# A hybrid decoder block on one core: the order of the FFN's products, where P2 of a block stands and when its sum is added

## The chip, the cores and the metric

One core of one Trainium2 chip runs the whole block in one launch. The metric is the device time of one execution in microseconds. Below, PE is TensorE, DVE VectorE, ACT ScalarE, POOL GpSimd and SP SyncE, whose queue starts nearly all DMAs.

## The reference, cut to what matters

The block is a decoder layer over 1024 tokens of width 1024. Its first part (two kinds of linear attention, an output projection, layer norms) is not touched. The part that matters is the second, a gated MLP whose up-projection is followed by a causal convolution of three taps along the tokens:

```python
def conv_ffn(h, w_up, conv_w, conv_b, w_down):
    u = causal_dwconv(h @ w_up, conv_w) + conv_b
    gate, val = jnp.split(u, 2, axis=-1)
    return (jax.nn.silu(gate) * val) @ w_down

x = layer_norm(ALPHA * x + (1.0 + gt_a) * y, ln1_g[l], ln1_b[l])
h = x * (1.0 + sc_f) + sh_f
y = conv_ffn(h, ffn_w_up[l], ffn_conv[l], ffn_conv_b[l], ffn_w_down[l])
x = layer_norm(ALPHA * x + (1.0 + gt_f) * y, ln2_g[l], ln2_b[l])
```

`w_up` is 1024 x 5632 (2816 gate columns, 2816 value columns), `w_down` 2816 x 1024, all in float32.

## The kernel before, in words

Float32 products are made of three matmuls each: every operand is split into a high and a low part (`hi`, `lo`; ACT casts the high part, DVE or POOL subtracts it to get the low one), and PE adds hi x lo, lo x hi and hi x hi. On top of that a product of 2 x 2 blocks is made with seven block products P1 to P7 in place of eight, whose operands and results are sums of blocks.

**First product (up).** `w_up` is worked through in 22 blocks f = 0 to 21, each of 128 gate columns and 128 value columns. `product(f, i)` (L1281) is 12 matmuls of 128x512. A block has two PSUM tiles named `up`, `gp[f]` for the gate and `vp[f]` for the value, each with two halves of 512 columns and two buffers, so that `gp[f]` reuses the buffer of `gp[f-2]`. P1, P6 and P7 go to half 1 of `gp[f]`, P2 to half 0; P5 and P3 go to half 0 of `vp[f]`. P4 of block f goes on top of P7 in half 1 of `gp[f]` and is computed only in the middle of block f+1. "A pair" below is the stretch in which PE does P1(f), P5(f), P4(f-1) and the other four products of f.

`carry` does what follows each product on the other engines. Behind P1, P5 and P6 an ACT copy puts the bank into SBUF cells (`p1_`, `p5_`, `u2_`; L1471, L1473, L1475). `add_p1` (L1458, DVE) adds the copy of P1 to half 0 of `gp[f]`, where P2 lies. Behind P3 and P7 come DVE sums (L1479, L1481), behind P7 also the value's convolution: one ACT pass (L1400) and two DVE passes (L1403). Behind P4(f-1) `gate_end(f-1)` does the gate's convolution (the same three passes), the silu (ACT, L1462) and the multiply of gate and value (DVE, L1463, 1024 columns). A wait is for a whole tile: a product that writes half 1 of `gp[f]` also waits for an `add_p1(f)` that was issued ahead of it and touches half 0 only. P2 waits for the copy `p1_`, P7 for the copy `u2_`.

The weights of block f+1 are prepared meanwhile. `load_w` starts the DMAs (L1326, L1327 for the value, L150 in `gate_block` for the gate, 512 KB). `weights` forms the sums on DVE (L1333, L1336, L1346, L1347) and splits them (`split_q`, L1306). `split_w` splits the gate's block: an ACT cast (L157, into `whi`) and a POOL subtraction over 1024 columns (L158, into `wlo`); `whi` and `wlo` have two buffers, which P1 and P2 of a block read, P2 last. Every second pair `sums` forms the operands of the second product and stores them to DRAM (`put_split`: L1410 cast, L1411 subtraction, L1412 and L1413 stores); `residual_rows` works on the residual (L1451, L1452).

**The first seam.** `h2_of(t)` makes row block t of the FFN's input: PE transposes (L1224), then ACT and DVE (L1231 to L1245) scale, split and sum them. P1 and P2 of blocks 0 and 1 are computed between the last of these, then P4(0), P5(0) and so on, whose left operands (`s1h` to `s4l`, L1362 and L1363) are sums over all row blocks.

**Second product (down).** The same seven products, 11 steps each, all steps of one product before the next, in `ORDER`. `b_of` loads and forms the right operand in `R0`, `R1` or the ring `bt`; `collect` takes each finished product out of PSUM. P4 comes last, and `ln2` does the last layer norm on row blocks.

The order of PE's instructions is written out by hand (`seq`, `ORDER`). On the other engines a scheduler orders the instructions when the program is built, so the place of a DVE instruction is read from the built program and not from the source. `tc.issue_after` fixes single instructions behind another.

Of the kernel before, what the change touches and what calls it, by code (L numbers as in the profile page):

```python
# [16 lines left out]
ALU = mybir.AluOpType  # L17
# [8 lines left out]
NT = 8  # L26
DFF = 2816
NF = DFF // P
# [59 lines left out]
def build(ctx, tc, out, cst, x, c, ln0_g, ln0_b, w_ada, b_ada, w_in, dn_conv, dn_a_log, dn_dt_bias,  # L88
# [1198 lines left out]
    with tc.manual_schedule(engines={PE.engine}):  # L1287
        for t in range(NT):
            y_half(t, 1)
            ln1(t)  # L1290
            if t >= LAG:
                h2_of(t - LAG)
        raw = {0: gate_block(0), 1: gate_block(1)}
        product(0, 1)
        product(0, 2)
    mix.close()
# [68 lines left out]
    with tc.manual_schedule(engines={PE.engine}):  # L1365
# [3 lines left out]
        next(ahead)  # L1369
        h2_of(NT - 2)  # L1370
        product(1, 1)
        next(ahead)
        for i, tag in ((5, "s1"), (6, "s2"), (3, "s4"), (7, "s3")):
# [4 lines left out]
            opA[i] = (lambda k, hl=parts_s[i]: tuple(a[:, :, ct(k)] for a in hl))  # L1378
        h2_of(NT - 1)
        product(1, 2)  # L1380
        for i in (5, 6):
# [56 lines left out]
    def residual_rows(n):  # L1438

        hf, t = n // NT, n % NT  # L1440
        if t == 0:
            for box, v, tag in ((g1h, ln1_g, "g1h"), (b1h, ln1_b, "b1h")):
                box[0] = ft([P, 512], tag, 1)
                nc.sync.dma_start(box[0], v[0][HS[hf]].partition_broadcast(P))
                S.mul(box[0], box[0], ALPHA)
        r = r_cells[n % 2]
# [7 lines left out]

    pending, anchor = [], [None]

# [10 lines left out]
    def carry(f, i):  # L1467
# [4 lines left out]
        elif i == 5:  # L1472
            S.copy(p5_, v[:, 0, :])  # L1473
        elif i == 6:
            S.copy(u2_, g[:, 1, :])  # L1475
        elif i == 2 and f < NF - 1:
            add_p1(f)
# [21 lines left out]
    with tc.manual_schedule(engines={PE.engine}):  # L1499
# [11 lines left out]
        for f in range(1, NF):  # L1511
            more = f + 1 < NF
            if f == 1:
                seq = (5, 6, 3, 7)
            elif more:
                seq = (2, -4, 6, 3, 7)
            else:
                seq = (-4, 6, 3, 7, 2)
# [40 lines left out]
    R0 = fr.tile([P, NJ, 512], F32, tag="R0", name="R0")  # L1559
    ORDER = (1, 5, 6, 3, 7, 2, 4)  # L1560
    SPARE = (NJ - 3, NJ - 2, NJ - 1)
# [6 lines left out]
    def b_of(i, j):  # L1568

        r0, r1 = R0[:, j, :], R1_[0][:, j, :] if R1_ else None  # L1570
        if i in (6, 3):
            b = dt_([P, 512], "bt", 6)
            load_b(b, j, 1, 1)
            if i == 3:
                return b
            V.tensor_tensor(r1, b, r1, op=ALU.subtract)
            return r1
        if i == 1:
            load_b(r0, j, 0, 0)
        elif i == 2:  # L1580
            load_b(r0, j, 1, 0)
        elif i == 5:
# [3 lines left out]
        elif i == 7:  # L1586
            V.tensor_tensor(r0, r1, r0, op=ALU.subtract)
        else:
            V.tensor_tensor(r0, r0, r1, op=ALU.subtract)
        return r0  # L1590
# [39 lines left out]
    def matmuls(pb, i, j, t, cols=slice(0, 512)):  # L1630
        hi, lo = ents[i, j]
        l_hi, l_lo, r_hi, r_lo = hi[:, ct(t)], lo[:, ct(t)], hi[:, HS[1]][:, cols], lo[:, HS[1]][:, cols]
        new = i in (1, 5, 2) and j == 0
        PE.matmul(pb, l_hi, r_lo, start=new, stop=False, skip_group_check=i not in (1, 5, 2))  # L1634
        PE.matmul(pb, l_lo, r_hi, start=False, stop=False, skip_group_check=i not in (1, 5, 2))  # L1635
        PE.matmul(pb, l_hi, r_hi, start=False, stop=(j == NJ - 1), skip_group_check=i not in (1, 5, 2))  # L1636

# [37 lines left out]
    def collect(i, t, pb):  # L1675
# [4 lines left out]
        elif i == 6:  # L1680
            S.copy(c12(t), pb)
        elif i == 3:
            done(c12(t), pb, HS[1], res[t, 1], c12(t))
            stats(t, HS[1], 512)
        elif i == 7:
            done(c22(t), pb, HS[1], res[t + 4, 1], c22(t))
            stats(t + 4, HS[1], 512 if t < 3 else 256)
        elif i == 2:
            done(c11(t), pb, HS[0], res[t, 0], c11(t))
            stats(t, HS[0], 512)  # L1690
            ln2(t, 2, CUT_EARLY)

    steps = [(i, j) for i in ORDER for j in range(NJ)]
    AHEAD = 5
    with tc.manual_schedule(engines={PE.engine}):
# [6 lines left out]
        for i in ORDER[:-1]:  # L1702
            pbs = on5 if i in (5, 3, 2) else on1
            for j in range(NJ):
                if n < len(steps):
                    entry(*steps[n])
                    n += 1
                if i == 3 and j == 0:
                    ln2_rows.extend(rows_of(2, ln2_g[0], ln2_b[0]))
# [41 lines left out]
```

## Time and profile before

| | us |
|---|---|
| median of 3 runs | 1446.52 (1445.31 to 1451.27) |
| profiled execution | 1447.39, of which the span is 1445.7 |
| PE busy | 1337.2 (92%) |
| DVE busy | 1005.0 (70%) |
| ACT busy | 590.1 (41%) |
| POOL busy | 532.9 (37%) |

Times below are counted from the start of the span. Busy time includes time in which a started instruction is held up by something else on the chip. The mean granted clock of TensorE was 0.956 of full speed.

### The profile page before, as it was taken

How to read it: one execution, taken by the hardware profiler on the slowest of the kernel's cores; microseconds unless marked ns; L12 is line 12 of the kernel's file. 1: busy time of each engine (PE TensorE's matmuls, PEld its weight loads, DVE VectorE, ACT ScalarE, POOL GpSimd, SP SyncE). 2: the span in 40 equal slices, each digit the busy share in tenths (PEclk: the TensorE clock that was granted, in tenths of full speed). 3: DMA queues.
4: the chain of work that ended last, by engine and by line, in shares of the span. 5: the costliest groups of instructions: out<-in, count | busy, mean ns of one | idle time of the engine just before them, and what ended most of it. 6: DMA issues, size and time to landing. Idle time of an engine off the chain costs nothing.

```text
span 1445.7 us, 19012 instructions
## 1 busy us (share of the span) xinstructions
PE 1337.2 (92%) x6662; PEld 1061.9 (73%) x6662; DVE 1005.0 (70%) x1770; ACT 590.1 (41%) x957; POOL 532.9 (37%) x369
## 2 busy tenths in 40 slices
PE   6796999999999899999988989999899998999995
PEld 4564768787887678777866767777687786788885
DVE  7885955487547432794497768877988887732777
ACT  4356222233234332352565444454544544353222
POOL 2674311122115667352323433444444331342006
PEclk9898999999999999899999999999999998999998
DMA  9557212122203464253132343445444438975773
GB/s 316 148 157 208 65 32 59 32 68 57 58 23 102 139 190 146 88 189 117 78 113 80 103 140 126 143 160 189 148 143 160 153 119 307 391 243 162 266 252 117
DMA packets 195572, 209.15 MB, mean 145 GB/s; under 512 B 30099, under 2 KB 125199, under 8 KB 195477
## 3 DMA queue, kind: packets, MB, share of 16 engines
q1 hardware_dynamic: 195189, 206.89, 44.5%
q8 instruction: 53, 0.87, 0.3%
q10 hardware_dynamic: 288, 1.05, 0.2%
q14 instruction: 42, 0.34, 0.1%
HBM read 149.92 MB, written 57.97 MB: 144 GB/s over the span
## 4 chain that ended last, share of the span: by engine, by line
PE 50%; DVE 23%; DMA 10%; issue 9%; POOL 4%; ACT 3%; SPq 1%; POOLq 0%; DVEq 0%; ACTq 0%
PE up L1281 9%; PE pp L622 6%; PE pp L623 5%; PE pp L624 5%; PE up L1634 4%; PE up L1636 4%; PE up L1635 4%; DMA vq<-in_ffn_w_up 3%; DVE ob L1403 2%; DVE vq L1333 1%; POOL vl L1306 1%; PE dn L864 1%; DVE mac L236 1%; DMA K<-in_w_ada 1%; DVE vl L1306 1%
## 5 line engine op out<-in xcount | busy, mean ns | idle before, releaser
L622 PE MATMUL pp<-aH,wlo 128*128 128x512 f32 x432 | 190.9, 442 | 8.8 <-DVE ob L651 6.4
L158 POOL TENSOR_TENSOR wlo<-wst,whi 128x1024 fp32r<-128x1024 f32 x50 | 122.6, 2452 | 160.0 <-ACT whi L157 159.5
L624 PE MATMUL pp<-aH,whi 128*128 128x512 f32 x432 | 176.8, 409 | 0.0
L623 PE MATMUL pp<-aL,whi 128*128 128x512 f32 x432 | 176.7, 409 | 0.0
L1306 POOL TENSOR_TENSOR vl<-vq,vh 128x512 fp32r<-128x512 f32 x44 | 70.2, 1595 | 213.3 <-ACT vh L1305 209.0
L1634 PE MATMUL up<-aL,aH 128*128 128x512 f32 (+1 forms) x304 | 118.7, 391 | 11.8 <-DVE ob L1669 7.1
L1403 DVE SCALAR_TENSOR_TENSOR ob<-up,colC,ob 128x1023 f32<-128x1023 f32 (+1 forms) x88 | 112.2, 1276 | 20.8 <-ACT ob L1400 19.5
L1635 PE MATMUL up<-aH,aL 128*128 128x512 f32 (+1 forms) x304 | 118.2, 389 | 0.0
L1636 PE MATMUL up<-aH 128*128 128x512 f32 (+1 forms) x304 | 118.2, 389 | 0.0
L622 PEld LDWEIGHTS pp<-aH,wlo 128*128 128x128 f32 x432 | 85.0, 197 | 30.7 <-DVE ob L651 5.1
L624 PEld LDWEIGHTS pp<-aH,whi 128*128 128x128 f32 x432 | 84.9, 196 | 20.6
L623 PEld LDWEIGHTS pp<-aL,whi 128*128 128x128 f32 x432 | 85.5, 198 | 14.5 <-issue 0.5
L1281 PE MATMUL up<-aH,wlo 128*128 128x512 f32 x176 | 74.0, 420 | 17.4 <-ACT ob L1471 14.1
L157 ACT CAST whi<-wst 128x1024 fp32r<-128x1024 f32 x50 | 52.3, 1046 | 82.6 <-DMA wst<-in_ffn_w_up 31.5
L1616 ACT CAST aH<-R 128x512 fp32r<-128x512 f32 x63 | 39.1, 621 | 100.7 <-PE up L1636 94.1
L1617 DVE TENSOR_TENSOR aL<-R,aH 128x512 fp32r<-128x512 f32 x63 | 44.1, 705 | 51.9 <-ACT aH L1616 51.8
L1634 PEld LDWEIGHTS up<-aL,aH 128*128 128x128 f32 x304 | 58.5, 192 | 24.5 <-DVE ob L1669 7.3
L1281 PE MATMUL up<-aH,vl 128*128 128x512 f32 x176 | 70.8, 402 | 5.8 <-DVE vl L1306 4.2
L1281 PE MATMUL up<-aH,whi 128*128 128x512 f32 x176 | 71.9, 409 | 0.0
L1281 PE MATMUL up<-aL,whi 128*128 128x512 f32 x176 | 71.7, 407 | 0.0
L1281 PE MATMUL up<-aL,vh 128*128 128x512 f32 x176 | 70.4, 400 | 0.0
L1281 PE MATMUL up<-aH,vh 128*128 128x512 f32 x176 | 70.1, 398 | 0.0
(520 smaller groups left out, 3395.6 us busy)
## 6 DMA issues: line engine op xcount, KB each, us to landing
wst<-in_w_in SPq DMA_DIRECT2D x28, 512.0 KB
K<-in_w_ada SPq DMA_DIRECT2D x48, 256.0 KB, 3.0
wst<-in_ffn_w_up SPq DMA_DIRECT2D x22, 512.0 KB
vq<-in_ffn_w_up SPq DMA_DIRECT2D x44, 256.0 KB, 3.1
R<-in_ffn_w_down SPq DMA_DIRECT2D x33, 256.0 KB, 5.4
wada<-in_w_ada SPq DMA_DIRECT2D x8, 1024.0 KB, 8.8
dS<-ob SPq DMA_DIRECT2D x22, 256.0 KB, 2.4
st<-dS SPq DMA_DIRECT2D x22, 256.0 KB, 3.9
```

Of the source, the lines that this page charges most:

```text
L157: S.copy(hi, st)
L158: eng.tensor_tensor(lo, st, hi.bitcast(F32), op=ALU.subtract)
L622: PE.matmul(pp, lo[:, k, :], aH[:, k, sl], start=(k == 0), stop=False)
L623: PE.matmul(pp, hi[:, k, :], aL[:, k, sl], start=False, stop=False)
L624: PE.matmul(pp, hi[:, k, :], aH[:, k, sl], start=False, stop=(k == NK - 1))
L1281: PE.matmul(o, w[:, k, :], a, start=flags[0], stop=flags[1], skip_group_check=not first_)
L1306: eng.tensor_tensor(lo, q, hi.bitcast(F32), op=ALU.subtract)
L1403: V.scalar_tensor_tensor(t[:, sh:], cb[:, :T - sh], w(j), t[:, sh:], op0=ALU.mult, op1=ALU.add)
L1617: V.tensor_tensor(lo[:, HS[1]], b, hi[:, HS[1]].bitcast(F32), op=ALU.subtract)
L1634: PE.matmul(pb, l_hi, r_lo, start=new, stop=False, skip_group_check=i not in (1, 5, 2))
L1635: PE.matmul(pb, l_lo, r_hi, start=False, stop=False, skip_group_check=i not in (1, 5, 2))
L1636: PE.matmul(pb, l_hi, r_hi, start=False, stop=(j == NJ - 1), skip_group_check=i not in (1, 5, 2))
```

## The change

There are three edits. In the first product the order of a pair on PE goes from P1 P5 P2 P4(f-1) P6 P3 P7 to P1 P5 P4(f-1) P2 P6 P3 P7, and from f = 2 to f = 20 `add_p1(f)` is issued behind P6 and its copy instead of behind P2. So P6 no longer waits for it, and P7 does. At the first seam the transposes and sums of row block 6 go ahead of P1(0), and P2(0) goes behind row block 7; one ACT scaling of a row (L1445) is fixed behind the copy of P5. In the second product the order goes from P1 P5 P6 P3 P7 P2 P4 to P1 P5 P6 P2 P7 P3 P4. There P3 no longer adds to P5's bank, which costs four DVE additions behind P6; P2's right operand goes through the ring `bt`, and P4 loads its block into `R0` again (11 more loads of 256 KB). The layer norm of the first four row blocks stays behind the sixth product.

```diff
--- before.py
+++ after.py
@@ -1290,9 +1290,9 @@
             ln1(t)
             if t >= LAG:
                 h2_of(t - LAG)
+        h2_of(NT - 2)
         raw = {0: gate_block(0), 1: gate_block(1)}
         product(0, 1)
-        product(0, 2)
     mix.close()
     ffn1 = ExitStack()
     fp = ffn1.enter_context(tc.tile_pool(name="ffn1", bufs=1, reuse_waits="tile"))
@@ -1367,7 +1367,6 @@
         ahead = weights(0)
         next(ahead)
         next(ahead)
-        h2_of(NT - 2)
         product(1, 1)
         next(ahead)
         for i, tag in ((5, "s1"), (6, "s2"), (3, "s4"), (7, "s3")):
@@ -1377,6 +1376,7 @@
             parts_s[i] = hi, ft([P, 4, 512], tag + "l", 1, F32R)
             opA[i] = (lambda k, hl=parts_s[i]: tuple(a[:, :, ct(k)] for a in hl))
         h2_of(NT - 1)
+        product(0, 2)
         product(1, 2)
         for i in (5, 6):
             for r0, r1 in ((0, 2), (2, 3), (3, 4)):
@@ -1442,7 +1442,8 @@
             for box, v, tag in ((g1h, ln1_g, "g1h"), (b1h, ln1_b, "b1h")):
                 box[0] = ft([P, 512], tag, 1)
                 nc.sync.dma_start(box[0], v[0][HS[hf]].partition_broadcast(P))
-                S.mul(box[0], box[0], ALPHA)
+                with tc.issue_after(anchor[1].ins):
+                    S.mul(box[0], box[0], ALPHA)
         r = r_cells[n % 2]
         d = ax2[t * P:(t + 1) * P, HS[hf]]
         nc.sync.dma_start(r, d)
@@ -1452,7 +1453,7 @@
             V.tensor_tensor(r, r, b1h[0], op=ALU.add)
         nc.sync.dma_start(d, r)
 
-    pending, anchor = [], [None]
+    pending, anchor = [], [None, None]
 
     def add_p1(f):
         V.tensor_tensor(gp[f][:, 0, :], gp[f][:, 0, :], p1_, op=ALU.add)
@@ -1470,10 +1471,12 @@
         if i == 1:
             S.copy(p1_, g[:, 1, :])
         elif i == 5:
-            S.copy(p5_, v[:, 0, :])
+            anchor[1] = S.copy(p5_, v[:, 0, :])
         elif i == 6:
             S.copy(u2_, g[:, 1, :])
-        elif i == 2 and f < NF - 1:
+            if 2 <= f < NF - 1:
+                add_p1(f)
+        elif i == 2 and f < 2:
             add_p1(f)
         elif i == 3:
             anchor[0] = V.tensor_tensor(v[:, 0, :], v[:, 0, :], u2_, op=ALU.add)
@@ -1513,7 +1516,7 @@
             if f == 1:
                 seq = (5, 6, 3, 7)
             elif more:
-                seq = (2, -4, 6, 3, 7)
+                seq = (-4, 2, 6, 3, 7)
             else:
                 seq = (-4, 6, 3, 7, 2)
             if more:
@@ -1557,7 +1560,7 @@
     ln2_rows = []
     stat2 = dt_([P, NT, 4, 6], "stat2")
     R0 = fr.tile([P, NJ, 512], F32, tag="R0", name="R0")
-    ORDER = (1, 5, 6, 3, 7, 2, 4)
+    ORDER = (1, 5, 6, 2, 7, 3, 4)
     SPARE = (NJ - 3, NJ - 2, NJ - 1)
     ents, spare2 = {}, []
     R1_ = []
@@ -1568,17 +1571,15 @@
     def b_of(i, j):
 
         r0, r1 = R0[:, j, :], R1_[0][:, j, :] if R1_ else None
-        if i in (6, 3):
+        if i in (6, 3, 2):
             b = dt_([P, 512], "bt", 6)
-            load_b(b, j, 1, 1)
-            if i == 3:
+            load_b(b, j, 1, int(i != 2))
+            if i != 6:
                 return b
             V.tensor_tensor(r1, b, r1, op=ALU.subtract)
             return r1
         if i == 1:
             load_b(r0, j, 0, 0)
-        elif i == 2:
-            load_b(r0, j, 1, 0)
         elif i == 5:
             load_b(r1, j, 0, 1)
             V.tensor_tensor(r1, r1, r0, op=ALU.subtract)
@@ -1586,6 +1587,7 @@
         elif i == 7:
             V.tensor_tensor(r0, r1, r0, op=ALU.subtract)
         else:
+            load_b(r0, j, 1, 0)
             V.tensor_tensor(r0, r0, r1, op=ALU.subtract)
         return r0
 
@@ -1630,10 +1632,10 @@
     def matmuls(pb, i, j, t, cols=slice(0, 512)):
         hi, lo = ents[i, j]
         l_hi, l_lo, r_hi, r_lo = hi[:, ct(t)], lo[:, ct(t)], hi[:, HS[1]][:, cols], lo[:, HS[1]][:, cols]
-        new = i in (1, 5, 2) and j == 0
-        PE.matmul(pb, l_hi, r_lo, start=new, stop=False, skip_group_check=i not in (1, 5, 2))
-        PE.matmul(pb, l_lo, r_hi, start=False, stop=False, skip_group_check=i not in (1, 5, 2))
-        PE.matmul(pb, l_hi, r_hi, start=False, stop=(j == NJ - 1), skip_group_check=i not in (1, 5, 2))
+        own = i in (1, 5, 2, 3)
+        PE.matmul(pb, l_hi, r_lo, start=own and j == 0, stop=False, skip_group_check=not own)
+        PE.matmul(pb, l_lo, r_hi, start=False, stop=False, skip_group_check=not own)
+        PE.matmul(pb, l_hi, r_hi, start=False, stop=(j == NJ - 1), skip_group_check=not own)
 
     c11 = lambda t: acc[:, t, HS[0]]
     c12 = lambda t: acc[:, t, HS[1]]
@@ -1679,16 +1681,17 @@
             S.copy(c22(t), pb)
         elif i == 6:
             S.copy(c12(t), pb)
+            V.tensor_tensor(c12(t), c12(t), c22(t), op=ALU.add)
         elif i == 3:
             done(c12(t), pb, HS[1], res[t, 1], c12(t))
             stats(t, HS[1], 512)
+            ln2(t, 2, CUT_EARLY)
         elif i == 7:
             done(c22(t), pb, HS[1], res[t + 4, 1], c22(t))
             stats(t + 4, HS[1], 512 if t < 3 else 256)
         elif i == 2:
             done(c11(t), pb, HS[0], res[t, 0], c11(t))
             stats(t, HS[0], 512)
-            ln2(t, 2, CUT_EARLY)
 
     steps = [(i, j) for i in ORDER for j in range(NJ)]
     AHEAD = 5
@@ -1705,7 +1708,7 @@
                 if n < len(steps):
                     entry(*steps[n])
                     n += 1
-                if i == 3 and j == 0:
+                if i == 7 and j == 0:
                     ln2_rows.extend(rows_of(2, ln2_g[0], ln2_b[0]))
                 if j == 4:
                     for t in range(4):
```

Line numbers of the new program are one to three higher than the old: `add_p1` is L1459, the sums L1482 and L1484, the copies L1472, L1474 and L1476, silu and multiply L1463 and L1464.

On DVE, the rows of one pair in the middle of the first product, before. The gate tile of the pair is `up_7821`, that of the block before it `up_7677`; L1458 is `add_p1`, L1403 on `up_7677` the gate's convolution, L1463 the multiply:

```order
L1403 SCALAR_TENSOR_TENSOR ob<-up_7695,colC,ob 128x1022
L1458 TENSOR_TENSOR up_7821<-up_7821,ob 128x512
L1333 TENSOR_TENSOR vq_8013<-vq_8013,wst_8017 128x512
L1403 SCALAR_TENSOR_TENSOR ob<-up_7677,colC,ob 128x1023
L1306 TENSOR_TENSOR vl_7899<-vq_7849,vh_7898 128x512
L1403 SCALAR_TENSOR_TENSOR ob<-up_7677,colC,ob 128x1022
L1336 TENSOR_TENSOR vq_7849<-vq_7850,vq_7849 128x512
L1346 TENSOR_TENSOR ob<-wst_7853,vq_7849 128x512
L1479 TENSOR_TENSOR up_7835<-up_7835,ob 128x512
```

The same pair after the change, where the gate tile of the block before is `up_7681`:

```order
L1333 TENSOR_TENSOR vq_8013<-vq_8013,wst_8017 128x512
L1403 SCALAR_TENSOR_TENSOR ob<-up_7681,colC,ob 128x1023
L1306 TENSOR_TENSOR vl_7886<-vq_7849,vh_7885 128x512
L1403 SCALAR_TENSOR_TENSOR ob<-up_7681,colC,ob 128x1022
L1336 TENSOR_TENSOR vq_7849<-vq_7850,vq_7849 128x512
L1346 TENSOR_TENSOR ob<-wst_7853,vq_7849 128x512
L1464 TENSOR_TENSOR ob<-ob 128x1024
L1459 TENSOR_TENSOR up_7821<-up_7821,ob 128x512
L1306 TENSOR_TENSOR vl_7933<-vq_7849,vh_7932 128x512
```

`add_p1` stood ahead of the gate's convolution; now it stands behind that, behind two weight sums and behind the 1024-column multiply.

On ACT, the same pair before, from the copy of P5 to the silu:

```order
L1473 COPY ob<-up_7835 128x512
L1305 CAST vh_7893<-ob 128x512
L157 CAST whi_8019<-wst_8017 128x1024
L1400 ACTIVATE ob<-up_7677,colC 128x1024
L1305 CAST vh_7898<-vq_7849 128x512
L1475 COPY ob<-up_7821 128x512
L1462 ACTIVATE ob<-ob 128x1024
```

And after:

```order
L1474 COPY ob<-up_7835 128x512
L1305 CAST vh_7880<-ob 128x512
L1400 ACTIVATE ob<-up_7681,colC 128x1024
L1305 CAST vh_7885<-vq_7849 128x512
L157 CAST whi_8019<-wst_8017 128x1024
L1463 ACTIVATE ob<-ob 128x1024
L1476 COPY ob<-up_7821 128x512
```

The cast L157, on which POOL's L158 waits, went from ahead of the gate's convolution to behind it. It writes the buffer whose last reader is P2 of the same pair, and P2 now stands one product later.

On DVE at the first seam, before, the rows that end with the low part of P4(0)'s weights (`vl_6330`):

```order
L1336 TENSOR_TENSOR vq_6275<-vq_6276,vq_6275 128x512
L1363 TENSOR_TENSOR s2l_6339<-ob,s2h_6338 128x1024
L1239 TENSOR_TENSOR aL<-ob,aH 128x4x128
L1341 TENSOR_TENSOR vq_6327<-wst_6230,vq_6275 128x512
L1231 TENSOR_SCALAR gate<-dn_6355,AB_77 128x128 x4
L1306 TENSOR_TENSOR vl_6286<-vq_6275,vh_6285 128x512
L1242 TENSOR_TENSOR ob<-ob 128x512
L1458 TENSOR_TENSOR up_6242<-up_6242,ob 128x512
L1239 TENSOR_TENSOR aL<-gate,aH 128x4x128
L1306 TENSOR_TENSOR vl_6330<-vq_6327,vh_6329 128x512
```

And after, from the same weight sum to the same low part (`vl_6318` now):

```order
L1336 TENSOR_TENSOR vq_6288<-vq_6289,vq_6288 128x512
L1243 TENSOR_TENSOR ob<-ob 128x512
L1231 TENSOR_SCALAR gate<-dn_6343,AB_77 128x128 x4
L1245 TENSOR_TENSOR ob<-ob 128x512
L1341 TENSOR_TENSOR vq_6315<-wst_6255,vq_6288 128x512
L1363 TENSOR_TENSOR s1l_6325<-ob,aH 128x512
L1244 TENSOR_TENSOR ob<-ob 128x512
L1363 TENSOR_TENSOR s2l_6327<-ob,s2h_6326 128x1024
L1239 TENSOR_TENSOR aL<-gate,aH 128x4x128
L1306 TENSOR_TENSOR vl_6299<-vq_6288,vh_6298 128x512
L1459 TENSOR_TENSOR up_6267<-up_6267,ob 128x512
L1306 TENSOR_TENSOR vl_6318<-vq_6315,vh_6317 128x512
```

Two more rows stand between; counted from the last small row of the layer norm ahead (L1203), 17 DVE rows stood ahead of that low part and 20 do now.

## Rows read from the trace of the kernel before

**Rows 1.** Page: the span and busy time of each engine

```profile
span 1445.7 us, 19012 instructions
PE 1337.2 (92%) x6662; PEld 1061.9 (73%) x6662; DVE 1005.0 (70%) x1770; ACT 590.1 (41%) x957; POOL 532.9 (37%) x369
```

**Rows 2.** Stretches: seam, pairs f=2 to 20, second product (clock, DMA share, GB/s)

```profile
729.60:782.09 52.49, 43.20 (x176) 33.37 (x175) 48.15 (x66) 31.47 (x53) 14.77 (x8) 0.90 0.25 77
782.09:1184.46 402.37, 380.30 (x1597) 304.15 (x1596) 329.27 (x357) 195.32 (x280) 170.73 (x103) 0.98 0.42 141
1214.90:1432.00 217.10, 209.40 (x924) 172.91 (x924) 140.27 (x219) 74.63 (x128) 58.45 (x37) 0.98 0.73 256
```

**Rows 3.** Who PE waited for, 782 to 1184: us, times, longest

```profile
PE up L1281 <- ACT ob L1471: 14.1, 8, 2.5
PE up L1281 <- DVE up L1458: 6.5, 3, 3.2
```

**Rows 4.** PE in time: a pair without stalls (start, us, idle before)

```profile
872.92 0.39 PE L1281 MATMUL up<-aH,wlo 128*128 128x512 f32 x1
...
875.50 0.40 PE L1281 MATMUL up<-aH,whi 128*128 128x512 f32 x1
875.73 0.40 PE L1281 MATMUL up<-aH,vl 128*128 128x512 f32 x1
...
889.58 0.40 PE L1281 MATMUL up<-aL,vl 128*128 128x512 f32 x1
...
892.36 0.39 PE L1281 MATMUL up<-aH,wlo 128*128 128x512 f32 x1
```

**Rows 5.** PE in time: first matmuls of products behind a stall

```profile
818.08 0.51 PE L1281 MATMUL up<-s2h,vl 128*128 128x512 f32 x1 [1.42 <-DVE up L1458]
818.42 0.40 PE L1281 MATMUL up<-s2l,vh 128*128 128x512 f32 x1
...
842.37 0.80 PE L1281 MATMUL up<-s2h,vl 128*128 128x512 f32 x1 [3.17 <-DVE up L1458]
842.96 0.63 PE L1281 MATMUL up<-s2l,vh 128*128 128x512 f32 x1
```

**Rows 6.** DVE in time, pair of the order rows above

```profile
968.38 2.53 DVE L1333 TENSOR_TENSOR vq<-vq,wst 128x512 f32<-128x512 f32 x1 [3.32 <-DMA vq<-in_ffn_w_up]
...
972.62 1.27 DVE L1403 SCALAR_TENSOR_TENSOR ob<-up,colC,ob 128x1022 f32<-128x1022 f32 x1
...
975.80 0.68 DVE L1451 TENSOR_TENSOR ob<-ob,g1h 128x512 f32<-128x512 f32 x1
976.40 2.31 DVE L1463 TENSOR_TENSOR ob<-ob 128x1024 f32<-128x1024 f32 x1
```

**Rows 7.** POOL in time, the same pair

```profile
967.96 2.39 POOL L158 TENSOR_TENSOR wlo<-wst,whi 128x1024 fp32r<-128x1024 f32 x1 [2.91 <-ACT whi L157]
976.15 1.48 POOL L1306 TENSOR_TENSOR vl<-vq,vh 128x512 fp32r<-128x512 f32 x1 [5.79 <-ACT vh L1305]
```

**Rows 8.** ACT in time, the same pair

```profile
966.84 1.05 ACT L157 CAST whi<-wst 128x1024 fp32r<-128x1024 f32 x1 [3.42 <-DMA wst<-in_ffn_w_up]
967.79 1.21 ACT L1400 ACTIVATE ob<-up,colC 128x1024 f32<-128x1024 f32 x1
...
973.98 1.06 ACT L1462 ACTIVATE ob<-ob 128x1024 f32<-128x1024 f32 x1 [4.00 <-DVE ob L1403]
```

**Rows 9.** Line L1413, the stores: who waited, time to landing

```profile
  POOL gate L1411: 26.1, 6
  POOL ob L1411: 14.2, 6
...
DMA to landing us min/median/max: 2.0/4.2/6.4
```

**Rows 10.** PE in time: the waits at the seam and at the first product's end

```profile
747.00 0.79 PE L1281 MATMUL up<-aH,vl 128*128 128x512 f32 x1 [4.16 <-DVE vl L1306]
...
1203.58 0.79 PE L1281 MATMUL up<-aH,wlo 128*128 128x512 f32 x1 [2.31 <-DVE up L1481]
```

## The prediction

> **What bounds the kernel now.** The page comes first: PE is busy 92% of the span, no other engine more than 70% [rows 1]. So what counts is where PE stands still or runs slowly. The table of stretches puts that in figures [rows 2]. The first product's pairs f = 2 to 20 are the stretch from the first matmul of P1(2) to that of P1(21), 402.37 us. A pair without a stall shows what it could be: P1 at 872.92, P5 2.81 later, P7 16.66 later, the next P1 after 19.44 [rows 4]. Nineteen such pairs take 369.4, so 33.0 us of the stretch are lost. The list of waits names most of it [rows 3]: 14.1 us in eight stalls in which P2 waits for the ACT copy of P1's bank, and 6.5 us in three in which P6 waits for `add_p1`; two small ones bring the waits to 22.0. The other 11.0 are matmuls at the lower clock behind a stall: behind one of 3.17 us a matmul takes 0.63 us and not 0.40, behind one of 1.42 us it is 0.40 from the second matmul on [rows 5].
>
> In the second product PE is busy 209.40 of 217.10 us at clock 0.98 [rows 2], so the order there has next to nothing to win.
>
> **The change, part by part.** All sums are against the profiled 1447.39, which is 0.9 above the median of the runs.
>
> *P2 behind P4.* The copy of P1 gets a whole product more of time, some 2.8 us. The longest of the eight stalls is 2.5 [rows 3], so all eight go. *`add_p1` behind P6.* P6's three stalls go as well. With both, and the slow matmuls behind them, the pairs give back 33.0.
>
> *What P7 now waits for.* This is the term that decides. The built order puts `add_p1` on DVE behind the gate's convolution, two weight sums and the 1024-column multiply, and P7 writes the same tile. I count from P1(f) = 0; the slots are P5 2.8, P4 5.6, P2 8.4, P6 11.2, P3 13.9, P7 16.66, and a product's last matmul ends 2.97 after its first starts [rows 4]. DVE's shown times overlap by about 0.08 (975.80 to 976.40 is 0.60 for a shown 0.68) [rows 6], so a 512-column sum is 0.60 and a convolution pass, shown as 1.27, 1.2.
>
> - P4(f-1) ends at 8.6. L1400 takes 1.2 [rows 8], L1403 1.2, the weight split 0.6, L1403 1.2: DVE is through at 12.8.
> - P2 ends at 11.4 and sets `whi` free. L157 takes 1.05 [rows 8], to 12.4; POOL's L158 then runs 2.39 [rows 7], from 12.5 to 14.9.
> - L1336 wants to start at 12.8, beside L158. What that does is in the rows: L1333 started 0.42 behind an L158, took 2.53 instead of 0.68, and ended 0.56 behind the end of L158; L1463 started beside a POOL subtraction, took 2.31, and ended 1.08 behind it [rows 6, 7]. So L1336 ends at 15.5, L1346 at 16.1, the multiply at 17.2, `add_p1` at 17.8. P7 starts at 17.9 instead of 16.66: a stall of 1.25.
> - The silu (1.06 [rows 8], queued behind L157) ends near 13.9 and doesn't bind.
>
> Before, L158 stood beside P6 too, but only the weight sum L1333 stood in it [rows 6, 7], which PE did not wait for.
>
> The Trainium skill (SBUF — State Buffer, "Who interferes with whom") says that a VectorE operation with two inputs in SBUF and a GpSimd operation that reads SBUF exclude each other for the whole instruction, and that issue order decides which one blocks. The rows of L1333 and L1463 bear this out. By that rule the multiply comes when it does above; if the two engines could run side by side, L1336 would end at 13.4 and `add_p1` at 15.8, and P7 would not wait.
>
> Which of the two comes first is close: 12.5 against 12.8. If L1336 came first, POOL would get in behind it (L1306 on POOL started under L1451 on DVE, and the multiply behind L1451 then waited for it [rows 6, 7]), and the stall would be some 1.6. Bounds for one pair: 0 (no holding) and 2.0 (L158 whole behind L1336, with one further hold by another POOL subtraction). I take 1.25 in the 18 pairs f = 2 to 19; block 20 has no L158 left. That is 22.5. At 1.25 the clock should hold, as it did behind 1.42 [rows 5].
>
> *Pairs with `sums`.* In every second pair POOL does a subtraction L1411 between its weight split and L158, and that L1411 waits for a store to land. Before, POOL waited 26.1 us in six and 14.2 in six for it; stores land in 2.0 to 6.4 us, 4.2 in the middle [rows 9]. With the middle value L158 is hardly later; I add 0.3 in nine pairs, 2.7. The late case is a rival.
>
> *The other waits of the new order.* P4(f-1) needs the value's sum of P7 (now L1484) a product earlier, at 5.6. Behind `add_p1` DVE has at most seven 512-column operations ahead of it and itself 0.6, so it ends some 5 us after `add_p1`, at 22.8, which is 3.4 ahead of P4's new slot (17.9 + 2.8 + 5.6 = 26.3). No cost; if DVE fell 3.4 behind, each us more would be one of PE. Since `add_p1` no longer stands ahead of L1333 the weights come free earlier and their loads too, which is off PE's path.
>
> *The seam.* The same work stands in another order on PE; 52.49 us of it hold 48.15 of DVE [rows 2], so DVE sets this stretch. P4(0) waits 4.16 for the low part of its weights [rows 10], and the built order puts three more DVE rows ahead of it: 3 x 0.60 = 1.8, plus what the transposes ahead of P1(0) and their ACT work add. The total of DVE's work does not change, so the lower bound is 0; the upper is 6, if all of row block 6 (seven or so rows of DVE with their ACT passes) comes in front. The first pair with a moved `add_p1` starts from this backlog and may stall longer. I take 4 for both together.
>
> *End of the first product.* P2(21) waits 2.31 for L1481, with slow matmuls behind it [rows 10]. It comes behind P7(21) as before, but the pair ahead leaves DVE less behind: -1.3, between 0 and -2.
>
> *Second product.* Four DVE additions of 0.6 and 2.9 MB of loads more: over 217 us at 256 GB/s and a DMA share of 0.73 [rows 2] that is 13 GB/s more, DVE is busy 140 of 217 us, and both lie under PE. The last product and the tail keep their order. 0, between -0.5 and +2 (a late reload of P4's operand).
>
> Sum: -33.0 + 22.5 + 2.7 + 4 - 1.3 + 0 = -5.1, so 1442.3 for the profiled execution, and 1441.4 when that stands 0.9 above the median as it does before. I predict **1441.4**.
>
> **The rivals.**
>
> *A, P7 doesn't wait.* If POOL does not hold DVE up in this place (L158 later, or the chain earlier by 1.3), the new stall vanishes: 1446.5 - 33.0 + 4 - 1.3 = 1416. For it: a margin of only 1.25 in a chain of ten steps. Against it: L158 can't come before P2 ends, and it is 2.39 long.
>
> *B, slower: the late store.* If the store of `dS5l` lands over about 5 us after its issue, POOL's L1411 itself runs until 13.9 and L158 from there to 16.3. L1336, held by both, ends at 16.9, `add_p1` at 19.3: a stall of 2.7 to 3.4. Behind such a stall the clock drops, and a product's 12 matmuls cost 0.2 us more each, 2.5 in all [rows 5]. Against the 1.55 counted for such a pair that is 4 us more, in all nine 1441 + 36 = 1477, in half of them 1459. It decides from about 5.0 us of landing; the middle is 4.2, the longest 6.4 [rows 9]. The same result comes if stalls of 1.25 in every pair do lower the clock: 18 x 1 to 2 us.
>
> *C, the change doesn't do what it says.* The stalls only move from P2 and P6 to P7 in full, or the seam takes what the pairs give: 1446 to 1449.
>
> **How the numbers follow.** Chances: the forecast 0.58, with its own range 1433 to 1452 (P7's stall from 0.9 to 1.6, the seam from 0 to 6); A 0.18; B 0.17; C 0.07. A measurement tells about 0.5% from no change here, 7.2 us, so faster means under 1439.3. Of the forecast's 0.58, 0.22 lie below that, 0.34 within, 0.02 above. Faster 0.22 + 0.18 = 0.40, same 0.34 + 0.06 = 0.40, slower 0.02 + 0.17 + 0.01 = 0.20. A range from 1418 to 1458 leaves out half of A and half of B, 2 in 10.
>
> **What will show it.** Right: no waits of P2 for the copy, none of P6; P7 waiting for L1459 in most pairs, 1.0 to 1.6 each, with L1336 or the multiply drawn out beside L158; the stretch from P1(2) to P1(21) at 395 to 398; P4(0) waiting about 6; the second product unchanged to 1 us. Wrong: no wait at P7 (A), waits of about 3 in every second pair and a clock under 0.98 there (B), or P4(f-1) waiting for L1484, which I gave 3.4 us of room.

## The result, and the profile after

The changed kernel takes 1469.51 us in the median (1468.27 to 1472.99, four runs); the ratio to the kernel before is 1.0151, with an interval of 1.0128 to 1.0174. It is 1.5% slower. The forecast was 1441.4 with a range up to 1458.

The profiled execution takes 1468.59 us. The page's first lines, with busy time and share of each engine, and beneath them the table of stretches (length; busy time of PE, its weight loads, DVE, ACT, POOL with counts; granted clock; DMA share; GB/s):

```profile
span 1466.8 us, 18972 instructions
PE 1340.1 (91%) x6662; PEld 1063.9 (73%) x6662; DVE 1024.1 (70%) x1774; ACT 591.3 (40%) x957; POOL 524.9 (36%) x369
```

```profile
729.19:778.96 49.77, 42.55 (x168) 32.40 (x166) 42.75 (x58) 25.23 (x40) 13.51 (x7) 0.90 0.23 69
778.96:1210.05 431.09, 388.58 (x1598) 309.18 (x1598) 338.16 (x360) 199.05 (x282) 167.00 (x103) 0.96 0.41 133
...
1238.00:1455.00 217.00, 209.94 (x933) 174.34 (x934) 157.52 (x228) 75.87 (x131) 56.00 (x38) 0.98 0.78 271
```

The first row runs from P1(0) to P1(2); 49.77 against 52.49 [rows 2] looks shorter, but transposes moved out of that stretch (the seam's own run below). The second row holds the loss. From P1(2) to P1(21) the pairs take 431.1 us in place of 402.4 [rows 2], 28.7 more, and the clock there is 0.96 and not 0.98. The other parts of the span make up the rest: the part ahead of the seam, where nothing was changed, was 5.0 shorter in this execution, the seam 1.8 longer (below), the end of the first product 2.6 and the second product 1.9 shorter. That is 21.0 of the 21.1 by which the span grew.

Whom PE waited for in the pairs (us in total, times, longest):

```profile
PE up L1281 <- DVE up L1459: 42.3, 18, 5.4
PE up L1281 <- DVE up L1484: 0.2, 1, 0.2
```

All waits of P2 for the copy and of P6 for `add_p1` [rows 3] are gone, and in their place stands what the forecast named, 18 waits of P7 for `add_p1`. But they add up to 42.3 us, not 25. In time they are 5.43 at f = 2 and 1.49 at f = 3; then they alternate: eight of 1.32 to 1.35 (f = 4, 6, ..., 18) and eight of 3.03 to 3.40 (f = 5, 7, ..., 19). One of each, on PE in time (start, us, idle before), with matmuls that follow:

```profile
1028.04 0.47 PE L1281 MATMUL up<-aL,vl 128*128 128x512 f32 x1 [1.35 <-DVE up L1459]
1028.35 0.39 PE L1281 MATMUL up<-s3l,vh 128*128 128x512 f32 x1
...
1050.76 0.47 PE L1281 MATMUL up<-aL,vl 128*128 128x512 f32 x1 [3.04 <-DVE up L1459]
...
1051.43 0.63 PE L1281 MATMUL up<-aL,vh 128*128 128x512 f32 x1
```

Behind the short wait a matmul takes 0.39 at once. Behind the long one it takes 0.63, for most of that product.

DVE in the pair with the short wait, f = 12. L1336 is started at 1022.75, when the convolution is through, and takes 2.60 for a sum of 0.60; `add_p1` is the last row:

```profile
1021.56 1.27 DVE L1403 SCALAR_TENSOR_TENSOR ob<-up,colC,ob 128x1022 f32<-128x1022 f32 x1
1022.75 2.60 DVE L1336 TENSOR_TENSOR vq<-vq,vq 128x512 f32<-128x512 f32 x1
1025.45 0.69 DVE L1346 TENSOR_TENSOR ob<-wst,vq 128x512 f32<-128x512 f32 x1
1026.06 1.22 DVE L1464 TENSOR_TENSOR ob<-ob 128x1024 f32<-128x1024 f32 x1
1027.20 0.69 DVE L1459 TENSOR_TENSOR up<-up,ob 128x512 f32<-128x512 f32 x1
```

And POOL beside it:

```profile
1022.39 2.41 POOL L158 TENSOR_TENSOR wlo<-wst,whi 128x1024 fp32r<-128x1024 f32 x1 [4.28 <-ACT whi L157]
```

L158 ends at 1024.80, L1336 0.55 later. This is the chain of the prediction, step by step, with L1336 held as L1333 was in [rows 6]: P5(12) started at 1012.65, so `add_p1` ends 15.2 behind it, where the prediction had 15.0 (17.8 less 2.8). The pair is 21.05 us long, from P5 to the next P5, and all eight pairs with the short wait take 21.02 to 21.05. That is 1.6 more than the 19.44 without a stall [rows 4], though PE's idle time is only 1.35.

DVE in the pair with the long wait, f = 13:

```profile
1042.63 0.69 DVE L1433 TENSOR_TENSOR ob<-ob 128x512 f32<-128x512 f32 x1 [2.81 <-POOL ob L1411]
1043.24 1.28 DVE L1403 SCALAR_TENSOR_TENSOR ob<-up,colC,ob 128x1023 f32<-128x1023 f32 x1
1044.43 1.92 DVE L1306 TENSOR_TENSOR vl<-vq,vh 128x512 fp32r<-128x512 f32 x1
1046.28 1.27 DVE L1403 SCALAR_TENSOR_TENSOR ob<-up,colC,ob 128x1022 f32<-128x1022 f32 x1
1047.47 0.68 DVE L1336 TENSOR_TENSOR vq<-vq,vq 128x512 f32<-128x512 f32 x1
...
1049.93 0.69 DVE L1459 TENSOR_TENSOR up<-up,ob 128x512 f32<-128x512 f32 x1
```

And what ACT and POOL did there:

```profile
1038.35 0.62 ACT L1410 CAST ob<-ob 128x512 fp32r<-128x512 f32 x1 [2.92 <-DMA dS5h<-ob]
1038.88 0.58 ACT L1474 COPY ob<-up 128x512 f32<-128x512 f32 x1
...
1039.88 1.21 ACT L1400 ACTIVATE ob<-up,colC 128x1024 f32<-128x1024 f32 x1
```

```profile
1040.06 1.29 POOL L1306 TENSOR_TENSOR vl<-ob,vh 128x512 fp32r<-128x512 f32 x1 [2.90 <-ACT vh L1305]
1041.30 1.30 POOL L1411 TENSOR_TENSOR ob<-ob 128x512 fp32r<-128x512 f32 x1
1043.41 2.40 POOL L158 TENSOR_TENSOR wlo<-wst,whi 128x1024 fp32r<-128x1024 f32 x1 [0.81 <-ACT whi L157]
```

ACT's pass over the gate ends at 1041.09, so the first L1403 could start there. It starts at 1043.24. Ahead of it in DVE's queue stands L1433, the last difference of the operand sums, which waits until POOL has done its L1411 at 1042.60. DVE is idle for 2.81 us, the last 1.5 of them with the convolution ready behind that row. The delay brings L1306 beside L158, which holds it for 1.3 more; L1336 then comes behind L158 and takes 0.68. This is the picture in seven of the eight pairs with the long wait; at f = 11 the first L1403 comes ahead of L1433.

Why POOL is late stands in the same rows. ACT's cast L1410 of the last operand sum waits 2.92 us for the store of `dS5h`, the high part of an earlier operand sum, issued 5.3 us before at 1033.05: the cast writes the buffer that this store reads. Behind the cast in ACT's queue stand the copy of P5 and a cast L1305; POOL's L1306 waits for that L1305, and L1411 stands behind L1306. In all eight pairs with the long wait the cast waits so, for 2.6 to 3.5 us, and starts 5.0 to 5.9 us after the store's issue. An estimate of what this wait does: in the pair f = 12, where ACT had no such wait, POOL's L1306 started 4.2 behind P5's first matmul (1016.83 and 1012.65). At that pace it would have started at 1037.9 here (P5 at 1033.70) and L1411 would have ended at 1040.5, before the convolution was ready.

### The profile page after: what moved, and what is told of

It reads as the page before. It is cut to its first block, busy times and chain, and to the rows that moved or that the text cites. A ratio compares the mean times of both kernels' runs of the same rounds, so it can differ in the third digit from the quotient of the medians.

```text
span 1466.8 us, 18972 instructions
## 1 busy us (share of the span) xinstructions
PE 1340.1 (91%) x6662; PEld 1063.9 (73%) x6662; DVE 1024.1 (70%) x1774; ACT 591.3 (40%) x957; POOL 524.9 (36%) x369
## 4 chain that ended last, share of the span: by engine, by line
PE 55%; DVE 25%; DMA 7%; issue 5%; POOL 4%; ACT 4%; SPq 0%; POOLq 0%; DVEq 0%; ACTq 0%
PE up L1281 10%; PE pp L622 6%; PE pp L623 5%; PE pp L624 5%; PE up L1636 4%; PE up L1637 4%; PE up L1638 4%; DVE ob L1403 3%; DVE vq L1336 2%; DVE ob L1464 1%; PE pp L1182 1%; PE pp L1183 1%; PE pp L1184 1%; DVE mac L236 1%; PE dn L864 1%
## 5 line engine op out<-in xcount | busy, mean ns | idle before, releaser
L158 POOL TENSOR_TENSOR wlo<-wst,whi 128x1024 fp32r<-128x1024 f32 x50 | 121.9, 2439 | 185.2 <-ACT whi L157 184.6
L1403 DVE SCALAR_TENSOR_TENSOR ob<-up,colC,ob 128x1023 f32<-128x1023 f32 (+1 forms) x88 | 112.3, 1278 | 42.1 <-ACT ob L1400 41.2
L1306 POOL TENSOR_TENSOR vl<-vq,vh 128x512 fp32r<-128x512 f32 x44 | 64.5, 1466 | 179.8 <-ACT vh L1305 179.8
L157 ACT CAST whi<-wst 128x1024 fp32r<-128x1024 f32 x50 | 52.4, 1048 | 79.9 <-PE pp L624 30.0
L1305 ACT CAST vh<-vq 128x512 fp32r<-128x512 f32 x89 | 54.8, 618 | 74.1 <-PE up L1281 37.2
L1281 PE MATMUL up<-aL,vl 128*128 128x512 f32 x88 | 41.6, 472 | 42.3 <-DVE up L1459 42.3
L1281 PE MATMUL up<-aL,vh 128*128 128x512 f32 x176 | 75.8, 431 | 0.0
L1281 PE MATMUL up<-aH,wlo 128*128 128x512 f32 x176 | 70.8, 402 | 1.5 <-DVE up L1484 1.5
```

The lines of the kernel that those rows point to most:

```text
L157: S.copy(hi, st)
L158: eng.tensor_tensor(lo, st, hi.bitcast(F32), op=ALU.subtract)
L1281: PE.matmul(o, w[:, k, :], a, start=flags[0], stop=flags[1], skip_group_check=not first_)
L1305: S.copy(hi, q)
L1306: eng.tensor_tensor(lo, q, hi.bitcast(F32), op=ALU.subtract)
L1403: V.scalar_tensor_tensor(t[:, sh:], cb[:, :T - sh], w(j), t[:, sh:], op0=ALU.mult, op1=ALU.add)
```

## The experiments

Ratios are to the kernel before, with 95% intervals. Edits to the kernel before come first, then edits to the changed kernel.

**The three parts, each alone.** Of the change's diff, `seam_alone` has the moved `h2_of(6)` and `product(0, 2)`, `down_alone` all that follows `ORDER`, and `pairs_alone` this, with the ACT scaling fixed behind the copy of P5:

```diff
-            S.copy(p5_, v[:, 0, :])
+            anchor[1] = S.copy(p5_, v[:, 0, :])
...
-        elif i == 2 and f < NF - 1:
+            if 2 <= f < NF - 1:
+                add_p1(f)
+        elif i == 2 and f < 2:
...
-                seq = (2, -4, 6, 3, 7)
+                seq = (-4, 2, 6, 3, 7)
```

> The kernel before with the new order of the pairs alone: P2 behind P4 of the last block, add_p1 behind P6. Theory: all of the loss sits here; the stretch from P1(2) to P1(21) loses 28.7 us in the changed kernel and the end of the first product gives back 2, so 1447 + 27 = 1474 (1469 to 1478), P7 waiting 1.3 in pairs without the operand sums and 3.0 in those with them. Rival: the long wait of the first such pair (5.43 us at f = 2) comes from the new seam; then it is under 3 here, and the time is some 4 us lower, 1470.

1473.64 us, ratio 1.0185 (1.0165 to 1.0204). The theory holds: the whole loss sits in the pairs (436.9 us), and P7 waits 5.8 at f = 2 here too, so that wait does not come from the new seam.

> The kernel before with the second product's new order alone. Theory: nothing, 1447 within 1.5 us: the 1.9 us by which the second product is shorter in the changed kernel come from its start, where the clock fell behind a wait before and did not after. Rival: the order itself is worth 2 us (1445) or the 11 more loads cost 2 (1449).

1446.00 us, ratio 1.0000 (0.9985 to 1.0015). The order of the second product costs and gives nothing.

> The kernel before with the first seam of the change alone: row block 6's transposes ahead of P1(0), P2(0) behind row block 7. Theory: the seam gains by itself what the changed kernel shows there, 49.77 us from P1(0) to P1(2) instead of 52.49, so about 3 us less than before: 1444, ratio 0.998. Rival, as the forecast had it: three more DVE rows ahead of P4(0) cost 2 to 4 us, 1449 to 1451, and the gain in the changed kernel came from something else (the f = 1 pair or the ACT scaling moved out of the way).

1446.75 us, ratio 1.0006 (0.9991 to 1.0022). The expected gain is not there. The reason was a badly chosen cut: the stretch from P1(0) to P1(2) is 50.30 here, but the transposes moved ahead of P1(0), out of the stretch, and PE waits for them there. PE in time, the last matmul of the projection, the transposes with their waits, and P1(2):

```profile
730.37 0.40 PE L1184 MATMUL pp<-qT,aH 128*128 128x512 f32 x1
730.60 1.03 PE L1224 MATMUL dn<-ident,ob 128*128 128x128 f32 x8
732.80 0.66 PE L1224 MATMUL dn<-ident,ob 128*128 128x128 f32 x4 [1.16 <-ACT ob L1228]
735.50 0.66 PE L1224 MATMUL dn<-ident,ob 128*128 128x128 f32 x4 [2.05 <-ACT ob L1228]
...
786.21 0.48 PE L1281 MATMUL up<-aH,wlo 128*128 128x512 f32 x1
```

From that last projection matmul to P1(2) it is 55.8 us here, 55.3 in the changed kernel and 53.5 in the kernel before (728.57 to 782.09). But the stretch differs from execution to execution: it is 53.2 to 55.0 in the four traces with the old seam and 54.7 to 56.8 in the nine with the new one. So the new seam gains nothing. What it costs, some 1.3 us between the means, hardly stands out from that spread, and the time can't show it.

**P2 behind P4 and nothing else.**

```diff
-                seq = (2, -4, 6, 3, 7)
+                seq = (-4, 2, 6, 3, 7)
```

> The kernel before with P2 behind P4 of the last block and nothing else: add_p1 stays issued behind P2, so that P6, which comes right behind P2, waits for it. Theory: P2 no longer waits for the copy of P1, but P6 waits in every pair, since add_p1 can't start before P2 ends and stands behind a convolution pass on DVE: 0.7 to 2 us in each of 18 pairs, with the clock at risk: 1450 to 1465. Rival: DVE is free just then and P6 waits 0.7 each: 1440 or less, and moving add_p1 was the mistake.

1477.39 us, ratio 1.0215 (1.0183 to 1.0248). PE's waits in the pairs:

```profile
PE up L1281 <- DVE up L1458: 41.5, 19, 4.8
```

P6 waits in every pair, from f = 4 on 1.08 in those without operand sums and 2.1 to 4.7 in those with them: more than expected. So moving `add_p1` was not the mistake; with the other engines' queues as they are, this order costs PE whichever product waits for it. The interval overlaps with that of `pairs_alone`, so which place of `add_p1` is the better one isn't shown.

**The last difference of the operand sums behind `add_p1`**, in the changed kernel; nothing else on DVE changes its place in such a pair:

```diff
         put_split(2, j, a12, G)
-        yield
-        V.tensor_tensor(a12, a12, a11, op=ALU.subtract)
+        for _ in range(5):
+            yield
+        with tc.issue_after(anchor[2].ins):
+            V.tensor_tensor(a12, a12, a11, op=ALU.subtract)
```

where `anchor[2]` is the instruction of `add_p1`.

> The changed kernel with one instruction moved: the last difference of the operand sums (L1433, one 512-column subtraction on DVE in every second pair) is issued behind add_p1 instead of ahead of the gate's convolution. Theory: P7's wait of 3.0 in those pairs is 1.3 from the POOL subtraction L158 and 1.7 from this row, which holds the whole DVE queue until POOL is done with an L1411. Then P7 waits 1.3 in all pairs, the clock no longer drops behind it, and the time falls by 8 x 1.7 for the waits and some 12 for slow matmuls, to about 1444 (1440 to 1450). Rival, as the forecast's case B had it: the store lands late and holds L1411 and L158; then this row costs nothing and the time stays at 1468 to 1471 with waits of 3.0.

1447.35 us, ratio 1.0006 (0.9993 to 1.0018): 22 us less than the changed kernel, from one row of 0.6 us. The waits in the pairs, and the stretch:

```profile
PE up L1281 <- DVE up L1461: 28.3, 18, 5.5
```

```profile
782.98:1186.91 403.93, 375.57 (x1598) 299.42 (x1597) 342.57 (x360) 199.08 (x282) 170.75 (x103) 1.00 0.43 142
```

From f = 3 on, every wait is 1.32 to 1.38, and the clock is 1.00. So the 3.04 was 1.33 and 1.71, as expected. The path of rival B, a late L158, is out: in the pair shown above L158 started 12.5 us behind P1(13), where the prediction had it. A late store is not out. Here too ACT's cast L1410 waits for `dS5h`, 1.9 to 3.4 us in the same eight pairs, and with L1433 out of the way P7 does not feel it. So the long wait needs this row ahead of the convolution. That the store is what makes the row late is argued from the rows above; no run takes the store's delay alone out of the changed kernel.

**The gate weights' split behind the copy of P6**, in the changed kernel (`after_late_split`) and together with the move above (`late_split`):

```diff
-        hi, lo = split_w(st, [P, NK, P])
+        if f > 2:
+            with tc.issue_after(anchor[3].ins):
+                hi, lo = split_w(st, [P, NK, P])
+        else:
+            hi, lo = split_w(st, [P, NK, P])
...
-            S.copy(u2_, g[:, 1, :])
+            anchor[3] = S.copy(u2_, g[:, 1, :])
```

> The changed kernel with the gate weights' split (ACT cast L157, POOL subtraction L158) issued behind the copy of P6 in every pair, so that L158 runs behind the sums on which P7 waits and not beside them; the last difference of the operand sums stays where the change has it. Theory: the 1.33 of P7's wait is L158 holding DVE back. Then P7 waits nothing in the pairs without operand sums, and about 1.7 in those with them (the row that waits for POOL's L1411 is still ahead of the gate's convolution): the time falls by 18 x 1.3 to 1.6 and some of the slow matmuls, to 1430 to 1440. Rival: the wait comes from the length of the chain on DVE itself (multiply and weight sums ahead of add_p1); then L158's place changes nothing, waits of 1.3 and 3.0 stay and the time is 1469.

1448.80 us, ratio 1.0022 (1.0006 to 1.0038). P7 waits in 13 pairs, not 18:

```profile
PE up L1285 <- DVE up L1463: 25.4, 13, 3.1
```

Of the eight waits of 1.33 three are left at 0.25 to 1.08, five are gone. So L158's hold on DVE was that wait: L1336 takes 0.68 or 0.69 in all pairs here, and 2.59 or 2.60 in those eight of the changed kernel. But the pairs with operand sums wait 2.2 to 3.1, not the 1.7 that I expected, so the time is 9 us above the top of what I gave. L1433 waits only 0.2 to 0.7 there and comes behind the first L1403; the cast that waits for its store, 2.5 to 3.3 us, stands ahead of ACT's pass over the gate.

> Both moves together: the changed kernel with the last difference of the operand sums behind add_p1 and the gate weights' split behind the copy of P6. Theory: no wait of P7 left in the pairs from f = 3 on, a pair takes 19.44 as in the stall-free ones of before, and of the changed order's waits only the first pair's 5.5 us and P2(21)'s 1.3 stay: 1447 - 17 x 1.58 = 1420 (1416 to 1426), 1.8% under the kernel before. Rival: DVE, the next busiest, then has no slack and P4 or P2 waits for it instead: 1435 or more.

1439.30 us, ratio 0.9946 (0.9929 to 0.9962), faster than the kernel before. The theory held for the pairs without operand sums (seven of eight wait 0.2 or nothing, one 1.72), and failed for those with them:

```profile
PE up L1285 <- DVE up L1465: 19.1, 11, 2.2
```

There P7 still waits 1.6 to 2.2. The rival's number fits, its cause doesn't: neither P4 nor P2 waits in these pairs. ACT in time in such a pair shows the cast that waited in the changed kernel already (L1414 is L1410 here, L1404 the gate's pass L1400):

```profile
1064.19 0.62 ACT L1414 CAST gate<-ob 128x512 fp32r<-128x512 f32 x1 [2.76 <-DMA dS5h<-gate]
...
1065.72 1.21 ACT L1404 ACTIVATE ob<-up,colC 128x1024 f32<-128x1024 f32 x1
```

The cast waits for a store to land and holds ACT's queue ahead of the gate's pass.

**One row of the first pair behind the gate's convolution.**

```diff
-        V.tensor_tensor(B12, B12, st[:, KH[0], :], op=ALU.subtract)
+        with (tc.issue_after(g_conv[1].ins) if f == 4 else ExitStack()):
+            V.tensor_tensor(B12, B12, st[:, KH[0], :], op=ALU.subtract)
```

where `g_conv[1]` is the last pass of the gate's convolution in the pair f = 2.

> As the run with both moves, and one more row moved: the weight sum L1333 of block 4, which stands ahead of the gate's convolution in the pair f = 2 and waits there for a load until 4 us after that convolution could start, is issued behind it. Theory: this load is what makes P7(2) wait 5.4 us; the wait falls under 1.5 and the time by 4 to 6 against the run with both moves: 1415. Rival: the wait at f = 2 is a backlog of the seam on DVE; then it stays over 4 and the time does not move.

1436.43 us, ratio 0.9934 (0.9910 to 0.9959). P7(2) waits nothing, and the pair f = 2 takes 19.59 in place of 22.84. But in `late_split` that wait was 1.8 already, of 5.4: L1333 was no longer held by L158 (0.69 long in place of 2.63), and its load let it start 2.1 us sooner behind P1(2). The time falls by 2.9 and not by the 4 to 6 that I gave, and the intervals of the two runs overlap.

**The cast that waits for the store behind the gate's pass.**

```diff
-        put_split(2, j, a12, G)
-        for _ in range(5):
+        for _ in range(3):
+            yield
+        with tc.issue_after(a_conv[0].ins):
+            put_split(2, j, a12, G)
+        for _ in range(2):
             yield
```

where `a_conv[0]` is ACT's pass over the gate. POOL's subtraction and the two stores of that operand sum move with the cast.

> As the run with the first pair's row moved, and one put_split more moved: the ACT cast of the last operand sum (L1410), which waits in every second pair for the store of the one before it and holds the ACT queue ahead of the gate's convolution, is issued behind that convolution. Theory: the waits of P7 of 1.6 to 2.2 that are left in the pairs with operand sums come from that cast; they go to under 0.5, the pairs f = 2 to 20 take 375 to 380 us in place of 395, and the time falls to 1420 (1416 to 1426). Rival: those waits come from POOL's and DVE's subtractions of the operand sums, which only move; then P7 still waits 1.5 or more there and the time stays at 1434 to 1438.

1426.17 us, ratio 0.9856 (0.9825 to 0.9886): the fastest of all, 1.4% under the kernel before and 3% under the changed one. Waits and stretch:

```profile
PE up L1285 <- DVE up L1471: 13.6, 11, 3.2
```

```profile
781.91:1168.30 386.39, 372.81 (x1597) 298.70 (x1596) 346.12 (x358) 190.78 (x280) 177.81 (x103) 1.00 0.45 148
```

The direction is shown: the waits in the pairs with operand sums fall to 0 to 1.6, but for one of 3.2. Whether the cast alone did it is not, since the subtraction and the stores moved with it. The 3.2 stands at f = 11, where L1333 (L1340 here) waits 2.6 for a DMA ahead of the convolution. Several waits of about 1 stay, so the stretch is 386 and not 380; what they wait for was not followed up.

**The old order of the pairs with the same moved rows.** The last kernel with `seq` and the place of `add_p1` as before.

> The last kernel with its four moved rows, seam and second product, but with the pairs in the order of the kernel before: P2 ahead of P4 of the last block and add_p1 behind P2. Theory: the changed order of the pairs is worth something once its own waits are gone: here P2 waits for the copy of P1 in some eight pairs again, and P6 for add_p1 in some, and the stretch of the pairs is 395 to 403 and the time 1440 to 1446. Rival: the moved rows cure the old order as well; then the time is 1426 or less and the new order of the pairs is worth nothing.

1437.02 us, ratio 0.9931 (0.9910 to 0.9952), below the range that I gave but far from the rival's 1426, with one block's difference formed from overwritten data, as the next expectation says.

> The run before this one again, with the last difference of the operand sums issued one step earlier: in the run before, in the last pair only, that difference came behind the convolution that overwrites its operand, so that one block's difference had other data. Theory: the time does not move, 1437 (1433 to 1441), against 1426 with the new order of the pairs. Rival: 1430 or less, and the difference between the two orders was that row.

1435.29 us, ratio 0.9925 (0.9896 to 0.9955). The old waits are back:

```profile
PE up L1285 <- ACT ob L1483: 12.8, 10, 2.4
PE up L1285 <- DVE up L1470: 4.2, 2, 2.3
```

So the moved rows help the old order as well, by 0.75%, and with them the new order is worth some 9 us more (the intervals of the two ratios just don't overlap). In the kernel as it was changed, it cost more than that.

## Why the prediction was wrong, point by point

- **The pairs' loss of 33.0 goes away**: right. No wait of P2 for the copy or of P6 for the sum is left. But not all of the 11.0 beyond the waits was the lower clock: the pair f = 3, whose wait of 1.42 left the clock up [rows 5], is 21.13 long, 1.69 over 19.44.
- **P7 now waits behind the gate's chain, 1.25 a pair**: the mechanism was right, and its cause: with L158 moved, five of the eight short waits go and three shrink. The price was too low. The idle time is 1.32 to 1.35, and each of these pairs is 0.26 longer than that, which makes 5 us in 18 pairs. L1336 waited out all of L158, 2.60 us for a sum of 0.60. The Trainium skill (SBUF — State Buffer, "Who interferes with whom") says that a VectorE operation with two inputs in SBUF contends with a GpSimd operation that reads SBUF. The trace agrees.
- **Pairs with `sums`, 0.3 more each**: this step failed. I looked for the late row on POOL, between its weight split and L158, and asked only whether L158 is late by it. The row that counts stands on DVE: L1433 waits for POOL's L1411 and stands ahead of the gate's convolution, at the head of the very chain that I had summed up. Measured, it is 1.7 in seven pairs and 2.1 at f = 11, 14 us, and with it the waits grow from 1.3 to 3.0 and more. `late_diff` shows it.
- **At 1.25 the clock should hold**: right for 1.25, but the step did not have waits of 3. Behind six of the eight waits of 3.0 to 3.4 and behind the 5.4 at f = 2, P7 took 4.3 to 5.5 us in place of 3.0, together 13.5 us. Without the row L1433 it is only the one at f = 2.
- **The seam and the first pair, 4 together**: P4(0) waited 3.35 and not about 6. The seam was 1.8 longer, by PE's waits for the transposes and within the spread of executions. The first pair was mis-sized: 5.4 us, from a load that L1333 waits for and from L158 which then holds L1333.
- **P4(f-1) has room ahead of L1484**: right, 3.3 to 5.1 us from f = 3 on; at f = 2 it waited, for 0.2.
- **End of the first product -1.3, second product 0**: -2.6 and -1.9 in these two executions. The 1.9 can't be put down to the change: over all traces the second product takes 229.0 to 230.8 in the old order and 228.2 to 230.5 in the new one.
- **Rival A** is out, since P7 waits in all 18 pairs, and the loss is larger than rival **C** had it.
- **Rival B** gave 1459 to 1477 for waits of 2.7 to 3.4 in the pairs with `sums` and the clock behind them. The waits, the pairs and the clock came as it said, and the time fell in its range. Its path was another: in the pair shown above, the store `dS5l` was issued at 1036.43 and had landed when POOL came to L1411, and L158 was not late. But a store later than "about 5 us" there was, the one of `dS5h`, and by the rows of that pair it worked through ACT's cast, POOL and DVE's L1433. I had read landing times of L1413's stores alone [rows 9]; `dS5h` is stored by L1412.

In sum, against the 1442.3 for the profiled execution, the pairs took 36 us more than forecast: 12 of waits beyond what I counted in the pairs with `sums`, 14 from the clock behind waits, 5 from the start behind each of the 18 waits, 4 at f = 2, and 1 in small parts. The seam gave back 2, the end of the first product and the second product 3, and the unchanged part ahead of the seam 5, which was luck; that leaves the 26 by which the profiled execution missed.

## What to carry to other kernels

When a wait moves to another instruction, write out the whole queue ahead of the new releaser, and for each row in it the engine that it waits for, and follow that engine's queue back too; a short row that waits for a third engine can cost its wait and not its length, as L1433 did. Cut stretches for comparison at instructions that the change moves nothing across: a cut at P1(0) showed a gain of 3 us where there was none. And before giving up a reordering that lost, look at what is left in the new chain: here four moves turned +1.5% into -1.4%.

## What the runs showed of the hardware that I had not expected

- A POOL subtraction over 1024 columns (2.40) beside a DVE sum over 512 made the sum 2.60 long, in all eight pairs without operand sums (waits of 1.32 to 1.35); I had expected more spread.
- The clock did not fall behind any of the 25 waits of 1.32 to 1.38 in the changed kernel and in `late_diff`. Behind waits of 3.0 it fell six times and twice not, in pairs that look alike (3.06 at 868.36 and 3.03 at 1141.15 without a drop). In `late_split` it fell behind waits of 1.81 and 1.97 too and held behind one of 2.22.
- A wait cost more than the idle time that the profile shows, at the full clock too: in `late_diff`, the 17 pairs from f = 3 to 19 are 0.25 to 0.27 us longer than 19.44 and the wait together. About 0.16 of that comes from how the profile shows it: a matmul is 0.39 long there while the next one starts 0.23 behind it [rows 4].
